# Wider weight casts and subtractions, and a shorter step of the S5 scan, in a two-layer hybrid diffusion step

## The chip, the core and the metric

The kernel runs on one core of one Trainium2 chip. The metric is device time in microseconds (us), the median of timed runs. TensorE (PE) multiplies matrices, VectorE (DVE) and ScalarE (ACT) do elementwise work, GpSimd (POOL) does small setups and issues DMAs, and SP issues the DMAs of the weights.

## The reference

The reference is one inference step of a small model with two layers, a width of 2048, and two streams of 128 tokens each (context and latent). All data are float32. Each layer does:

```python
h = rms_norm(x, norm_w) * (1 + scale) + shift          # adaLN: shift, scale, gate = c @ w_mod
hg..., at..., s5_u, s5_g, merge = split_columns(h @ w_in)   # 2048 x 15872
o_hg = hgrn2(...)          # gated linear recurrence, both directions
o_at = attention(...)      # 8 query heads, 2 key heads
o_s5 = s5(...)             # diagonal complex state space, both directions, 64 groups x 64 states
merged = g_hg * (o_hg @ w_br_hg) + g_at * (o_at @ w_br_at) + g_s5 * (o_s5 @ w_br_s5)
x = x + gate * (merged @ w_out)
```

The S5 branch runs, in each direction, `state[t+1] = a * state[t] + b[t]` with complex numbers; the new states of all branches are outputs too.

## The kernel before

**Weights.** Every large product goes through `gemm` (line 160). A weight matrix comes from HBM in pieces of 128 x 1024 float32 (512 KB), which hold two chunks of 128 rows by 512 columns. SP loads a piece into `raw` (three buffers, line 167). For each of the two halves, ScalarE casts it to the matmul's format, `wh`, and VectorE subtracts, `wl = raw - wh`, the remainder (`split_from`, lines 137 to 139). There are four buffers of 512 columns for each of `wh` and `wl` (the pool `weights`, line 68). PE then does six matmuls of 512 columns with a half: for each of the two streams lo x wh, hi x wh and hi x wl (lines 178 to 180), where hi and lo are the two parts of the activations, split in the same way. Sums stand in PSUM.

**The order.** Instructions carry priorities (the constants `P_...`, where a lower number goes first), and a planner of the framework lays down at build time the order of each engine, by its own estimate of when each instruction is ready. The order is then fixed. HGRN2 and attention come first (`P_MIX`), then the scan (`P_SCAN`), then the weights' loads, casts and subtractions (`P_TOP`), the layer's chain of small steps (`P_CHAIN`), the rest of S5 (`P_S5`), and last the weight matmuls (`P_PE`). The products of adaLN (`mod_part`, line 272) run as side work between weight matmuls: four column blocks of 256 side by side in the array, with weights of their own (`wm`), also loaded by SP.

**The S5 scan.** `s5_quarter` (line 782) does a quarter of the groups at a time. Two tokens are one step, so there are NP = 64 steps, over 8 quarters in the two layers: 512 steps. The states of both directions, real and imaginary parts, are 64 numbers a partition. A step (lines 822 to 831) has four VectorE operations, all 64 wide: the states times the real part of the coefficient (line 825), the swapped states times the signed imaginary part (line 827), the sum of both products (line 830), and the addition to the next input (line 831). The coefficients stand in a table `s5sc` of 384 numbers that `s5_params` writes once a layer (lines 693 to 703). `p` is a ring of four buffers for the products.

Ahead of a quarter's scan POOL sets up: it negates one half of C (line 791), copies four blocks into CC (line 762) and copies the initial state (line 804).

Of the kernel before, what the change touches and what calls it, by code (L numbers as in the profile page):

```python
# [11 lines left out]
F32R = mybir.dt.float32r  # L12
# [3 lines left out]
ALU = mybir.AluOpType  # L16
# [45 lines left out]
class Builder:  # L62
    def __init__(self, tc, ctx, io):
        self.tc, self.nc, self.io = tc, tc.nc, io
        self.seq = 0
        pool = lambda name, bufs, **kw: ctx.enter_context(tc.tile_pool(name=name, bufs=bufs, **kw))
        self.cp = pool("const", 1)
        self.wp = pool("weights", 4)
        self.sb = pool("sb", 1)
        self.bufs = dict(H8=4, Z8=2, Bl=1, CC=1, S16=1, uT=1, U2=1, ys=1, q4=2, kv=2,  # L70
                         mo=1, st=10, k2=6, k4=3, gt=4, sm=18, s5i=4, p=4, sb=1, sc=1, s5t=1)
        self.pg = pool("pg", 4, space=PSUM)
        self.pm = pool("pm", 2, space=PSUM)
        self.pb = pool("pb", 2, space=PSUM)
        self.dr = pool("scratch", 1, space=DRAM)
        self.uid = 0
# [51 lines left out]

# [1 line left out]
    def transpose4(self, src, n=4, ps=None):  # L130
# [29 lines left out]
    def gemm(self, pieces, hi, lo, nk):  # L160
        """hi(k), lo(k): [128, 256] stationary parts of both streams; pieces: DRAM APs [128, 1024]."""
        nc = self.nc
        ps = [self.pg.tile([128, 512], F32, tag="g", name=self.nm("g")) for _ in range(2)]
        for kk, src in enumerate(pieces):
            self.side_work()
            with self.prio(P_TOP):
                raw = self.wp.tile([128, 2, 512], F32, tag="raw", name=self.nm("raw"), bufs=RAW)
                nc.sync.dma_start(raw, src.rearrange("p (a b) -> p a b", a=2))
            for j in range(2):
                with self.prio(P_TOP):  # L170
                    wh = self.wp.tile([128, 512], F32R, tag="wh", name=self.nm("wh"))
                    wl = self.wp.tile([128, 512], F32R, tag="wl", name=self.nm("wl"))
                    self.split_from(raw[:, j], wh, wl)
                k = 2 * kk + j
                with self.prio(P_PE):
                    for s in range(2):
                        sl = slice(s * 128, s * 128 + 128)
                        nc.tensor.matmul(ps[s], lo(k)[:, sl], wh, start=(k == 0), stop=False)  # L178
                        nc.tensor.matmul(ps[s], hi(k)[:, sl], wh, start=False, stop=False)  # L179
                        nc.tensor.matmul(ps[s], hi(k)[:, sl], wl, start=False, stop=(k == nk - 1))  # L180
        return ps

    def rstd(self, ssq, n, width):
        """1/sqrt(ssq/width + eps), with one Newton step after the table's square root."""
        nc = self.nc
# [12 lines left out]

# [1 line left out]
    def condition(self):  # L200
# [41 lines left out]

# [1 line left out]
    def mod_part(self, l, part, prio, tags, plan):  # L244
        """A sixth of c @ w_mod for both streams, two k chunks at a time; four column blocks side by side.

        Parts 0 to 3 are shift and scale of a quarter of the channels, 4 and 5 the halves of the gate. plan: runs
        of chunk pairs that are summed in PSUM, (bank, pairs, pairs between two yields)."""
        nc, io = self.nc, self.io
# [46 lines left out]

# [1 line left out]
    def square(self, ssq, x, s, n):  # L298
# [9 lines left out]
    def normed(self, x, rs, q):  # L308
        """Channels 512 q .. 512 q + 511 of both streams."""
        nc = self.nc  # L310
# [20 lines left out]
    def in_group(self, l, name, idx, k0=0, k1=16):  # L331
        """Channel chunks k0 .. k1 - 1 of one group of columns."""
        pieces = [self.io["w_in"][l, GIDX[name, idx], kk] for kk in range(k0 // 2, k1 // 2)]
# [7 lines left out]
    def begin(self, l, name, idx, q):  # L341
        """A quarter of the channels' share of a group, put where the whole will stand."""
        ps = self.in_group(l, name, idx, 4 * q, 4 * q + 4)
# [40 lines left out]

# [1 line left out]
    def hgrn_unit(self, l, s, hf, q, f, v, og):  # L386
        """Four heads of one stream. q, f[2] (sigmoids), v: [128 tokens, 512]; og: output slice [128, 512].

        Pairs (s, t) are covered by a binary tree over time: at level m the queries of one half of every
        2m-block meet the keys of the other half; QF/KB carry the decay from the block's inner edge."""  # L390
        nc, io = self.nc, self.io
# [97 lines left out]

# [1 line left out]
    def head_norm(self, x, nh, w):  # L491
# [22 lines left out]
    def attention(self, l, s, q, kv, og):  # L514
        """q: [128, 8, 128], kv: [128, 512] (2 key heads, 2 value heads); og: [128, 1024]."""
        nc, io = self.nc, self.io
# [57 lines left out]

# [1 line left out]
    def vexp(self, x, n, wk):  # L576
        """exp on the vector engine to float32 accuracy."""
        nc = self.nc
# [60 lines left out]
    def s5_params(self, l):  # L639
        """Discretised per-state coefficients of both directions.  # L640

        The scan runs over pairs of tokens: state' = a^2 state + (a B u_first + B u_second)."""
        nc, io = self.nc, self.io
# [48 lines left out]
        cmul(acr, aci, abr, abi, cr, ci)  # L692
        sc = self.const(f"s5sc{l}", (128, 384))
        o = lambda off, ds: view(sc, off, ds)
        for qd in range(4):
            for d in range(2):
                i = qd * 2 + d
                pm = lambda c: view(c, d * 32 + qd * 8, [[1, 2], [2, 2], [4, 2]])
                for ri in range(2):
                    nc.vector.tensor_copy(o(i * 16 + ri * 8, [[4, 2], [2, 2], [1, 2]]), pm(a2r))  # L700
                    for st in range(2):
                        ts(o(128 + i * 32 + ri * 16 + st, [[8, 2], [4, 2], [2, 2]]), pm(a2i), 2.0 * ri - 1.0, None, ALU.mult)
        self.s5sc[l] = sc

    def s5_input(self, l, qd, Bl, C, Sb):
        """Input matrices of one quarter, block-diagonal over two groups, the odd token's part stacked on the
        even one's; built in the scan's buffer before the scan needs it."""
        nc, io = self.nc, self.io
# [34 lines left out]
    def s5_output(self, l, qd, C, CC, cb):  # L743
        """C a of both directions, and C B + diag(d), which joins a token to its own output."""
        nc = self.nc
# [18 lines left out]
    def s5_half(self, l, hh, us, ys):  # L764
        """Channels of chunks 4*hh .. 4*hh+3 of both streams; us[s]: [128 tokens, 512]."""
        nc = self.nc
# [15 lines left out]
    def s5_quarter(self, l, hh, qh, uT, U2, ys):  # L782
# [37 lines left out]
        with self.prio(P_SCAN):  # L820
            for i in range(NP):
                p0 = self.t("p", "p0", (128, 2, 32))
                p1 = self.t("p", "p1", (128, 2, 32))
                ds = DD + NP - 2 * i
                tt(p0.rearrange("p d (j s) -> p d j s", s=2), view(sc, qd * 32, [[16, 2], [1, 16], [0, 2]]),  # L825
                   view(Sb, i, [[ds, 2], [2 * W, 16], [W, 2]]), ALU.mult)
                tt(p1, view(sc, 128 + qd * 64, [[32, 2], [16, 2], [1, 16]]),  # L827
                   view(Sb, i + RI, [[ds, 2], [-RI, 2], [W, 16]]), ALU.mult)
                cur = view(Sb, i + 1, [[ds - 2, 2], [W, 32]])
                tt(p0, p0, p1, ALU.add)  # L830
                tt(cur, cur, p0, ALU.add)  # L831
        with self.prio(P_S5):
# [22 lines left out]

# [1 line left out]
    def layer(self, l, x, rs):  # L857
# [247 lines left out]
def _tiles(w, ncol):  # L1105
    """[K, N] -> [N/ncol, K/256, 128, 2*ncol]: 128-row chunks in pairs, side by side."""
    k, n = w.shape
# [4 lines left out]
def _mod_parts(w):  # L1112
    """Columns shift | scale | gate -> quarters of shift and scale together, halves of the gate."""
    h = D // 4
# [91 lines left out]
```

## Time and profile before

| | before |
|---|---|
| median of 3 timed runs | 2419.5 us (2418.51 to 2420.97) |
| span of the profiled execution | 2418.4 us (the page gives no time beside the span) |
| instructions | 38199 |
| PE busy | 2355.8 us, 97% |
| VectorE busy | 1812.5 us, 75% |
| ScalarE busy | 1185.1 us, 49% |
| POOL busy | 132.9 us, 5% |
| casts of weights (line 138) | 1344, 823.1 us |
| subtractions for weights (line 139) | 1344, 916.0 us |
| four operations of the scan (lines 825, 827, 830, 831) | 512 each; 140.1, 138.2, 112.8, 140.8 us |

All rows come from one profiled execution. Busy time is the time in which an engine has an instruction in work. Matmuls overlap: a 512-wide one shows about 0.40 us, and the next starts 0.23 us after it. A wait names the instruction that waited and what released it.

### The profile page before, as it was taken

Reading aid. Unit: us, or ns where it says so; the run is one execution under the profiler, and the core shown is the slowest. Engines: PE = TensorE matmul, PEld = TensorE weight load, DVE = VectorE, ACT = ScalarE, POOL = GpSimd, SP = SyncE. Lnnn points to the kernel's source line nnn. Section 1 sums busy time; section 2 is a strip of 40 time slices with the busy share of each in tenths; the row PEclk is TensorE's granted clock in tenths of the full one; section 3 lists DMA queues with packets and bytes.
Section 4 is the critical chain, followed back from the end, with each engine's and each line's share of the span. In section 5 each row is a group of like instructions: output and inputs, shape, how many; then the busy total and the mean of one; then the engine's idle time right before and its main releaser. Section 6 shows DMA issues by size and latency. Waiting matters only on the chain.

```text
span 2418.4 us, 38199 instructions
## 1 busy us (share of the span) xinstructions
PE 2355.8 (97%) x13192; PEld 1817.0 (75%) x13192; DVE 1812.5 (75%) x4835; ACT 1185.1 (49%) x2061; POOL 132.9 (5%) x244
## 2 busy tenths in 40 slices
PE   5999999999999999999998999999999999999997
PEld 2667878888786676677776888888888776687776
DVE  5855998799878768665565798899869868856555
ACT  3436645555553433444446555555564453354444
POOL 2000001000100100000010001000010010000000
PEclk9999999999999999999999999999999999999999
DMA  8994553345557767777864554354546656656665
GB/s 311 344 326 133 161 181 115 124 155 192 170 164 261 238 212 252 243 270 252 298 214 143 158 175 153 126 166 149 184 157 191 198 166 211 219 174 219 224 199 177
DMA packets 131490, 483.85 MB, mean 200 GB/s; under 512 B 17200, under 2 KB 17808, under 8 KB 126944
## 3 DMA queue, kind: packets, MB, share of 16 engines
q1 hardware_dynamic: 120528, 454.09, 57.0%
q0 software_dynamic: 9472, 23.97, 3.4%
q10 hardware_dynamic: 1296, 3.36, 0.4%
q8 instruction: 103, 1.69, 0.3%
q14 instruction: 91, 0.75, 0.1%
HBM read 474.36 MB, written 6.98 MB: 199 GB/s over the span
## 4 chain that ended last, share of the span: by engine, by line
PE 92%; DMA 3%; DVE 3%; issue 1%; ACT 1%; SPq 0%; DVEq 0%; ACTq 0%
PE g L178 26%; PE g L180 25%; PE g L179 25%; PE mod L272 5%; PE bu L813 2%; PE lv L429 2%; DMA raw<-w_in 2%; PE tr L134 2%; PE yp L844 1%; DVE wl L139 1%; DMA wm<-w_mod 1%; PE yp L837 1%; PE bt L731 1%; PE ao L569 0%; PE sc L553 0%
## 5 line engine op out<-in xcount | busy, mean ns | idle before, releaser
L138 ACT CAST wh<-raw 128x512 fp32r<-128x512 f32 x1344 | 823.1, 621 | 1005.9 <-PE g L179 759.5
L139 DVE TENSOR_TENSOR wl<-raw,wh 128x512 fp32r<-128x512 f32 x1344 | 916.0, 688 | 418.2 <-ACT wh L138 365.6
L178 PE MATMUL g<-wh,hl 128*128 128x512 f32 x1984 | 798.2, 402 | 4.9 <-ACT wh L138 2.4
L179 PE MATMUL g<-wh,hh 128*128 128x512 f32 x1984 | 787.4, 397 | 0.0
L180 PE MATMUL g<-wl,hh 128*128 128x512 f32 x1984 | 716.6, 404 | 0.0
L178 PEld LDWEIGHTS g<-wh,hl 128*128 128x128 f32 x1984 | 375.1, 189 | 117.7 <-ACT wh L138 17.8
L180 PEld LDWEIGHTS g<-wl,hh 128*128 128x128 f32 x1984 | 366.0, 189 | 97.4 <-DVE Sb L831 6.6
L179 PEld LDWEIGHTS g<-wh,hh 128*128 128x128 f32 x1984 | 375.3, 189 | 81.8 <-issue 0.4
L272 PE MATMUL mod<-wm,cs 128*32 128x256 f32 x1536 | 155.6, 406 | 22.8 <-DMA wm<-w_mod 16.2
L178 PE MATMUL g<-wh,ol 128*128 128x512 f32 x384 | 154.5, 402 | 0.0
L825 DVE TENSOR_TENSOR p<-s5sc,Sb 128x64 f32<-128x64 f32 x512 | 140.1, 274 | 16.1 <-ACT Sb L817 7.1
L179 PE MATMUL g<-wh,oh 128*128 128x512 f32 x384 | 150.1, 391 | 0.0
L831 DVE TENSOR_TENSOR Sb<-Sb,p 128x64 f32<-128x64 f32 x512 | 140.8, 275 | 8.7
L827 DVE TENSOR_TENSOR p<-s5sc,Sb 128x64 f32<-128x64 f32 x512 | 138.2, 270 | 0.0
L180 PE MATMUL g<-wl,oh 128*128 128x512 f32 x384 | 133.9, 394 | 0.0
L272 PEld LDWEIGHTS mod<-wm,cs 128*32 128x32 f32 x1536 | 50.0, 113 | 106.8 <-issue 54.9
L830 DVE TENSOR_TENSOR p<-p,p 128x64 f32<-128x64 f32 x512 | 112.8, 220 | 6.4
L178 PE MATMUL g<-wh,mt 128*128 128x512 f32 x256 | 101.6, 397 | 0.0
L179 PE MATMUL g<-wh,mt 128*128 128x512 f32 x256 | 101.1, 395 | 0.0
L178 PEld LDWEIGHTS g<-wh,ol 128*128 128x128 f32 x384 | 72.0, 188 | 26.1 <-ACT wh L138 7.7
L180 PE MATMUL g<-wl,mt 128*128 128x512 f32 x256 | 85.4, 400 | 1.2 <-DVE wl L139 1.2
L180 PEld LDWEIGHTS g<-wl,oh 128*128 128x128 f32 x384 | 71.2, 188 | 18.7 <-DVE Sb L831 1.6
(315 smaller groups left out, 2112.6 us busy)
## 6 DMA issues: line engine op xcount, KB each, us to landing
raw<-w_in SPq DMA_DIRECT2D x496, 512.0 KB, 3.8
wm<-w_mod SPq DMA_DIRECT2D x130, 512.0 KB, 5.1
raw<-w_br SPq DMA_DIRECT2D x96, 512.0 KB, 4.2
raw<-w_out SPq DMA_DIRECT2D x64, 512.0 KB, 4.4
wm<-w_mod SPq DMA_DIRECT2D x31, 1024.0 KB, 7.4
raw<-w_glu SPq DMA_DIRECT2D x16, 512.0 KB, 4.3
gb<-gate_d POOLq DMA_DIRECT2D x16, 256.0 KB, 6.4
x<-x ACTq DMA_DIRECT2D x2, 1024.0 KB, 14.4
```

What stands on the lines that cost most here:

```text
L134: nc.tensor.transpose(ps[:, k], src[:, k * 128:(k + 1) * 128], self.ident)
L138: self.nc.scalar.copy(hi, src)
L139: self.nc.vector.tensor_sub(lo, src, hi.bitcast(F32))
L178: nc.tensor.matmul(ps[s], lo(k)[:, sl], wh, start=(k == 0), stop=False)
L179: nc.tensor.matmul(ps[s], hi(k)[:, sl], wh, start=False, stop=False)
L180: nc.tensor.matmul(ps[s], hi(k)[:, sl], wl, start=False, stop=(k == nk - 1))
L272: nc.tensor.matmul(ps[32 * i:32 * i + 32, 0:256], self.cT[:, 2 * k:2 * k + 32], ws[k - 2 * k0][:, i * 256:i * 256 + 256], start=(k == 2 * kb),
L429: nc.tensor.matmul(ps[:, h], mix[:, h], view(Z, HT + h * 128, [[2 * m, nb], [2 * HT + m, 2], [1, m]]), start=True, stop=True)
L825: tt(p0.rearrange("p d (j s) -> p d j s", s=2), view(sc, qd * 32, [[16, 2], [1, 16], [0, 2]]), view(Sb, i, [[ds, 2], [2 * W, 16], [W, 2]]) ...
L827: tt(p1, view(sc, 128 + qd * 64, [[32, 2], [16, 2], [1, 16]]), view(Sb, i + RI, [[ds, 2], [-RI, 2], [W, 16]]), ALU.mult)
L830: tt(p0, p0, p1, ALU.add)
L831: tt(cur, cur, p0, ALU.add)
```

## The change

The weights are cast and subtracted a whole piece at a time, 1024 wide, with three buffers for each of `wh` and `wl`; the matmuls read the halves of these. In the scan both products are one operation of 128 elements, whose inputs are read twice; the coefficient table is laid out for it (512 numbers), and its sum reads the second product with its halves swapped. The ring `p` has three larger buffers. The build call sets `dynamic_dma_scratch_size`. Comments are taken out. The core of the diff:

```diff
-        self.wp = pool("weights", 4)
+        self.wp = pool("weights", 3)
...
-                         mo=1, st=10, k2=6, k4=3, gt=4, sm=18, s5i=4, p=4, sb=1, sc=1, s5t=1)
+                         mo=1, st=10, k2=6, k4=3, gt=4, sm=18, s5i=4, p=3, sb=1, sc=1, s5t=1)
...
+            with self.prio(P_TOP):
+                wh = self.wp.tile([128, 2, 512], F32R, tag="wh", name=self.nm("wh"))
+                wl = self.wp.tile([128, 2, 512], F32R, tag="wl", name=self.nm("wl"))
+                self.split_from(raw, wh, wl)
             for j in range(2):
-                with self.prio(P_TOP):
-                    wh = self.wp.tile([128, 512], F32R, tag="wh", name=self.nm("wh"))
-                    wl = self.wp.tile([128, 512], F32R, tag="wl", name=self.nm("wl"))
-                    self.split_from(raw[:, j], wh, wl)
...
-                        nc.tensor.matmul(ps[s], lo(k)[:, sl], wh, start=(k == 0), stop=False)
+                        nc.tensor.matmul(ps[s], lo(k)[:, sl], wh[:, j], start=(k == 0), stop=False)
...
-        sc = self.const(f"s5sc{l}", (128, 384))
+        sc = self.const(f"s5sc{l}", (128, 512))
...
-                    nc.vector.tensor_copy(o(i * 16 + ri * 8, [[4, 2], [2, 2], [1, 2]]), pm(a2r))
                     for st in range(2):
-                        ts(o(128 + i * 32 + ri * 16 + st, [[8, 2], [4, 2], [2, 2]]), pm(a2i), 2.0 * ri - 1.0, None, ALU.mult)
+                        at = qd * 128 + d * 32 + ri * 16 + st
+                        nc.vector.tensor_copy(o(at, [[8, 2], [4, 2], [2, 2]]), pm(a2r))
+                        ts(o(at + 64, [[8, 2], [4, 2], [2, 2]]), pm(a2i), 1.0 - 2.0 * ri, None, ALU.mult)
...
-                p0 = self.t("p", "p0", (128, 2, 32))
-                p1 = self.t("p", "p1", (128, 2, 32))
+                p = self.t("p", "p", (128, 2, 2, 32))
                 ds = DD + NP - 2 * i
-                tt(p0.rearrange("p d (j s) -> p d j s", s=2), view(sc, qd * 32, [[16, 2], [1, 16], [0, 2]]),
-                   view(Sb, i, [[ds, 2], [2 * W, 16], [W, 2]]), ALU.mult)
-                tt(p1, view(sc, 128 + qd * 64, [[32, 2], [16, 2], [1, 16]]),
-                   view(Sb, i + RI, [[ds, 2], [-RI, 2], [W, 16]]), ALU.mult)
+                tt(p, view(sc, qd * 128, [[64, 2], [32, 2], [1, 32]]), view(Sb, i, [[0, 2], [ds, 2], [W, 32]]), ALU.mult)
                 cur = view(Sb, i + 1, [[ds - 2, 2], [W, 32]])
-                tt(p0, p0, p1, ALU.add)
-                tt(cur, cur, p0, ALU.add)
+                own = p[:, 0]
+                tt(own, own, view(p, 80, [[32, 2], [-16, 2], [1, 16]]), ALU.add)
+                tt(cur, cur, own, ALU.add)
...
-    nc = bacc.Bacc("TRN2", target_bir_lowering=False, num_devices=1)
+    nc = bacc.Bacc("TRN2", target_bir_lowering=False, num_devices=1, dynamic_dma_scratch_size=4096)
```

## Rows read from the trace of the kernel before

**Rows 1.** The page: span, then busy time, share and count of PE.

```profile
span 2418.4 us, 38199 instructions
...
PE 2355.8 (97%) x13192; PEld 1817.0 (75%) x13192; DVE 1812.5 (75%) x4835; ACT 1185.1 (49%) x2061; POOL 132.9 (5%) x244
```

**Rows 2.** Waits of PE, whole run: us in total, times, longest.

```profile
PE tr L134 <- DVE xn L319: 10.3, 3, 6.4
...
PE g L178 <- ACT wh L138: 2.4, 5, 1.2
...
PE g L180 <- DVE wl L139: 1.2, 2, 0.9
...
PE bu L813 <- ACT Bl L732: 0.4, 1, 0.4
```

**Rows 3.** Busy time of each engine in two windows, clock, DMA share.

```profile
700.00:750.00 50.00, 50.00 (x243) 38.55 (x241) 46.56 (x141) 23.87 (x41) 0.00 (x0) 1.00 0.70 228
...
1100.00:1150.00 50.00, 50.00 (x263) 37.45 (x260) 25.64 (x41) 20.28 (x35) 0.00 (x0) 1.00 0.77 253
```

**Rows 4.** Waits of ScalarE's casts, whole run.

```profile
ACT wh L138 <- PE g L179: 759.5, 834, 3.7
...
ACT wh L138 <- DMA raw<-w_in: 83.9, 35, 11.8
```

**Rows 5.** Groups by form: busy us, mean ns of one, then idle before.

```profile
L139 DVE TENSOR_TENSOR wl<-raw,wh 128x512 fp32r<-128x512 f32 x1344 | 916.0, 688 | 418.2 <-ACT wh L138 365.6 <-PE g L180 34.2 <-ACT Sb L817 2.8
L138 ACT CAST wh<-raw 128x512 fp32r<-128x512 f32 x1344 | 823.1, 621 | 1005.9 <-PE g L179 759.5 <-DMA raw<-w_in 83.9 <-DVE wl L139 58.2
...
L830 DVE TENSOR_TENSOR p<-p,p 128x64 f32<-128x64 f32 x512 | 112.8, 220 | 6.4
...
L501 DVE TENSOR_TENSOR q<-q,qnorm 128x1024 f32<-128x1024 f32 x4 | 4.9, 1220 | 0.0
```

**Rows 6.** Timeline of VectorE: one step of the scan (start, us, operation).

```profile
390.62 0.28 DVE L825 TENSOR_TENSOR p<-s5sc,Sb 128x64 f32<-128x64 f32 x1
390.81 0.27 DVE L827 TENSOR_TENSOR p<-s5sc,Sb 128x64 f32<-128x64 f32 x1
...
391.69 0.27 DVE L825 TENSOR_TENSOR p<-s5sc,Sb 128x64 f32<-128x64 f32 x1
```

**Rows 7.** Timeline: two subtractions and two casts of weights back to back.

```profile
304.19 1.27 DVE L139 TENSOR_TENSOR wl<-raw,wh 128x512 fp32r<-128x512 f32 x2
...
1256.71 1.14 ACT L138 CAST wh<-raw 128x512 fp32r<-128x512 f32 x2 [3.43 <-DMA raw<-w_out]
```

**Rows 8.** Timeline of PE: a short visit of adaLN between weight matmuls.

```profile
749.21 0.39 PE L178 MATMUL g<-wh,ol 128*128 128x512 f32 x1
749.44 0.39 PE L179 MATMUL g<-wh,oh 128*128 128x512 f32 x1
749.76 0.62 PE L272 MATMUL mod<-wm,cs 128*32 128x256 f32 x2
750.31 0.73 PE L180 MATMUL g<-wl,oh 128*128 128x512 f32 x2
```

**Rows 9.** Windows, line 272 alone: busy time of PE and PEld.

```profile
50.00:200.00 150.00, 25.70 (x384) 10.02 (x384) 0.98 0.82 294
...
700.00:1000.00 300.00, 48.46 (x416) 14.81 (x416) 1.00 0.72 237
...
1050.00:1250.00 200.00, 23.95 (x288) 9.05 (x288) 1.00 0.78 266
...
1900.00:2110.00 210.00, 26.45 (x160) 6.32 (x160) 1.00 0.61 199
```

**Rows 10.** Waits of the weight loader, first in 700:1000, then in 1900:2110.

```profile
PEld mod L272 <- issue: 16.6, 46, 0.4
...
PEld mod L272 <- issue: 14.5, 40, 0.4
```

**Rows 11.** Groups: the POOL operation on C, all eight.

```profile
L791 POOL TENSOR_SCALAR C<-C 128x256 f32<-128x256 f32 x8 | 10.9, 1364 | 6.7 <-DMA C<-s_c 6.6
```

**Rows 12.** Timeline of POOL: the first of these.

```profile
24.45 0.88 POOL L791 TENSOR_SCALAR C<-C 128x256 f32<-128x256 f32 x1
```

More of the change, by code (lines that the diff above doesn't have):

```diff
@@ L177, in gemm @@
                         sl = slice(s * 128, s * 128 + 128)
-                        nc.tensor.matmul(ps[s], lo(k)[:, sl], wh, start=(k == 0), stop=False)
-                        nc.tensor.matmul(ps[s], hi(k)[:, sl], wh, start=False, stop=False)
-                        nc.tensor.matmul(ps[s], hi(k)[:, sl], wl, start=False, stop=(k == nk - 1))
+                        nc.tensor.matmul(ps[s], lo(k)[:, sl], wh[:, j], start=(k == 0), stop=False)
+                        nc.tensor.matmul(ps[s], hi(k)[:, sl], wh[:, j], start=False, stop=False)
+                        nc.tensor.matmul(ps[s], hi(k)[:, sl], wl[:, j], start=False, stop=(k == nk - 1))
         return ps
@@ L696, in s5_params @@
             for d in range(2):
-                i = qd * 2 + d
                 pm = lambda c: view(c, d * 32 + qd * 8, [[1, 2], [2, 2], [4, 2]])
                 for ri in range(2):
-                    nc.vector.tensor_copy(o(i * 16 + ri * 8, [[4, 2], [2, 2], [1, 2]]), pm(a2r))
                     for st in range(2):
-                        ts(o(128 + i * 32 + ri * 16 + st, [[8, 2], [4, 2], [2, 2]]), pm(a2i), 2.0 * ri - 1.0, None, ALU.mult)
+                        at = qd * 128 + d * 32 + ri * 16 + st
+                        nc.vector.tensor_copy(o(at, [[8, 2], [4, 2], [2, 2]]), pm(a2r))
+                        ts(o(at + 64, [[8, 2], [4, 2], [2, 2]]), pm(a2i), 1.0 - 2.0 * ri, None, ALU.mult)
         self.s5sc[l] = sc
```

## The prediction

> **What bounds the kernel now.** I read the engines' busy times first, to see which engine has no slack: PE is busy 2355.8 of 2418.4 us [rows 1], so 62.6 us of the span are its idle time. The waits of PE say what for [rows 2]: 2.4 us for a cast weight (wh), 1.2 us for a weight remainder (wl), 10.3 us for the normalised input (xn) at the layers' starts; most of the rest is the first weights' arrival and what follows the last matmul. Waits for the two things that this change makes cheaper are therefore 3.6 us in 2418. Then the windows, for the share of VectorE by stage [rows 3]: 46.56 us of 50 where the S5 scan runs, 25.64 where it doesn't, and PE is at 50.00 in both. Last the waits of ScalarE [rows 4]: before 834 casts it stood 759.5 us until PE gave a weight buffer back, and only 83.9 us for a weight's DMA. Casts run ahead of PE and are held by PE, not PE by casts. PE's queue is the bound, and its length is the number of matmuls, the stalls, and what it costs to change from one kind of matmul to another.
>
> **The change part by part.**
>
> *Casts and subtractions 1024 wide.* 1344 casts and 1344 subtractions become 672 and 672. A subtraction of 512 takes 0.688 us alone [rows 5], two back to back 1.27 [rows 7]; a VectorE operation of 1024 on two float32 inputs took 1.22 [rows 5]. That saves 0.05 to 0.16 us a pair, 672 times: 34 to 104 us of VectorE. A cast of 1024 has no row. Below it lies 0.62 us (one of 512), above 1.24 (two of 512 apart); two back to back take 1.14 [rows 7], so the second adds 0.52, and I take 1.06, near that row. ScalarE is relieved by 672 x 0.08 = 54 us, by the bounds -67 to 417. All of this lies beside PE's matmuls, whose number and shape don't change: it is worth 0 on the path, except through the stalls and the order below.
>
> *The scan.* Four operations become three: two multiplications of 64 become one of 128, the two additions stay. A step now takes 1.07 us, from one first operation to the next (390.62 to 391.69 [rows 6]); the second multiplication starts 0.19 after the first. A 64-wide operation takes 0.220 and a 1024-wide one 1.220 [rows 5], 1.04 ns an element, so the wide multiplication adds 0.07 to the 0.28 of the first one. Bounds: 0 (one price for both) to 0.28 (twice the price). I take 0.07: 1.07 - 0.19 + 0.07 = 0.95, 0.12 us saved a step, 512 steps, 61 us of VectorE; by the bounds +0.19 to -0.09 a step, 97 us gained to 46 lost. The scan is not on PE's path: PE fills its time with weight matmuls meanwhile, so 0 again. If that cover were gone, the whole 61 us would count.
>
> *Three buffer pairs.* Four halves become three whole pieces, six halves. PE consumes a half in 6 matmuls, about 1.39 us (0.23 us from start to start [rows 8]); PE can go on for 8.3 instead of 5.6 us on what is cast when a weight comes late. The stalls for wh and wl (3.6 us) should nearly all go: -3, bounds -3.6 and 0.
> Against it stands the coarser grain: where the buffers ran empty, the first half waits for a cast of 1.06 instead of 0.62 and for a subtraction of 1.22 instead of 0.69, +0.44 to +0.97 an event. The seven waits in rows 2 would give +3 to +7 if the deeper buffers saved none; I take +1 for two that remain. Behind a wide subtraction on VectorE stand the operations that the layer's start needs (the longest wait for xn is 6.4 us [rows 2]); one that comes just behind it is 0.5 us later, and two layer starts have it: within the same +1. The raw buffers stay at three, so the first three DMAs of the run are the same. The smaller area named in the build call touches POOL's DMAs alone; they wait for engines, not for each other, and I cost it at 0 (one late gate load in the last column block would cost its whole delay).
>
> *The order on PE.* The planner lays PE's order down at build time, and it sees the new times. Here lies the largest term. The adaLN matmuls (line 272) are put between weight matmuls. In a run of 16 they cost 0.067 us each: 25.70 us for 384 in 50:200. In 700:1000 it is 48.46 for 416, in 1050:1250 23.95 for 288, in 1900:2110 26.45 for 160 [rows 9]. At 0.067 those 864 would take 57.9 us instead of 98.9: 41 us of PE go on short visits. In 1900:2110 the weight loader stood before such a visit 40 times, four matmuls a visit; in 700:1000 46 times [rows 10]. One visit shows where they come from [rows 8]: after the last matmul on wh (749.44) PE turns to two adaLN matmuls for 0.55 us, and only then to the two on wl. In the plan wl was late, and the gap was filled. Visits are short where VectorE is full by rows 3, longer in 1050:1250 where it is not. With one wl for 12 matmuls instead of one for 6, and a shorter scan step, there are fewer such gaps. Bounds: -41 us (all visits whole) and +44 (all 864 at the 0.165 of 1900:2110). I take -8, a fifth of the excess: only visits that stand between wh and wl can go, their matmuls must still run, and the planner may put other gaps in their place.
>
> **The sum.** -3 + 1 - 8 = -10 us on the profiled execution: 2408.4 us of span. The page gives that execution no time beside its span; the median of the timed runs (2419.5) is 1.1 us more. So 2409.5, rounded to 2410 us, 0.4% faster.
>
> **A rule of the skill that speaks against it.** A POOL operation that reads SBUF (line 791) took 0.88 us at 24.45 us, before VectorE had its first weight to subtract [rows 12], and 1.364 on average [rows 11]. The Trainium skill, "SBUF — State Buffer", section "Who interferes with whom", says that a VectorE instruction with two SBUF inputs blocks a GpSimd instruction that reads SBUF until it has finished. The trace agrees so far as the two figures differ by 0.48 us, less than one subtraction of 0.688; what this would give is the second rival below.
>
> **The rivals.**
> *PE-bound, order unchanged.* The relief of VectorE and ScalarE is hidden, the adaLN visits stay as they are, and 3.6 us of waits is all there was to win. For it: PE at 50.00 of 50, with VectorE full and with VectorE half idle. Against it: a planner that sees other times seldom gives the same order. -3 + 1 = -2: 2417.5 us. The same time comes out where the wide operations cost twice the narrow ones, so that the change doesn't do what it says.
> *A longer hold on VectorE that blocks POOL.* A wide subtraction lasts 0.53 us more than a narrow one. In each of the 8 S5 quarters seven POOL reads stand ahead of the scan or its output (the negation of C, four copies into CC, two of the initial state): 7 x 0.53 = 3.7 us later, 30 us in all if PE had run out of weight matmuls each time. It hasn't: of these I'd expect a third, +10, less 2 for the stalls and with no gain of order: 2427.5 us. It decides only from the point where PE waits for bu or yp; such a wait is 0.4 us in all today.
> *A worse order (slower).* The two casts' work comes in one lump of 12 matmuls, and the planner fills in adaLN, S5 and HGRN2 matmuls in more and shorter visits. Place: 700:1250 and 1900:2110. Price: the 2-matmul visit of rows 8 puts 0.87 us between two weight matmuls that otherwise start 0.23 apart, and two matmuls in a run of 16 take 0.13: 0.51 us for the visit itself. With 20 more such visits +10, less 2 for the stalls: 2427.5 us. It decides from 4 more visits on, where they cost the 2 us of the stalls. For it: each earlier gap was filled because a matmul was ready, and adaLN weights come in two halves. Against it: two wh come together now, so PE has eight matmuls to do before wl is missed, not four.
>
> **How the numbers follow.** Forecast 0.54; no change of order 0.24 (0.05 of it that wide operations save nothing); worse order 0.17; POOL blocked 0.05. About 0.2% (4.8 us) is what can be told from no change. The forecast's own range is 2397 to 2414: order terms of -20 to -4. The time falls below 2395 where more than half of the excess of 41 us goes, 0.08, and above 2427 in about half of the worse cases, 0.11; so 2395 to 2427. Faster: 0.54 less the part of the forecast that ends within 4.8 us, plus a little of the unchanged order that also gains: 0.54. Same 0.25, slower 0.21.
>
> **What would show it.** Line 139 at 1.22 us x672 and line 138 near 1.06 x672; a scan step of 0.95 us from start to start. PE's waits for wh and wl under 1.5 us together. PE's sum of waits otherwise as before, at the start, between the layers (6.4 us for xn) and behind the last matmul. Line 272 in the scan stages of both layers cheaper than 0.1165 and 0.165 us a matmul, and fewer than 46 and 40 waits of the weight loader before it. The order step is wrong if these counts stay or rise; then the gain is 2 us at most. The whole is wrong if VectorE's relief shows up as idle time of VectorE and PE's busy time grows.

## The result, and the profile after

| | before | after |
|---|---|---|
| median | 2419.0 us (4 runs beside these) | 2388.2 us (2385.4 to 2389.9, 4 runs) |
| ratio | | 0.9871, interval 0.9857 to 0.9885 |
| span of the profiled execution | 2418.4 us | 2388.1 us |
| span less PE's busy time | 62.6 us | 68.0 us |

The kernel became 1.3% faster. The direction was forecast, the size was not: 2410 was said, and 2388.2 lies below the range of 2395 to 2427.

The page of after, for [rows 1]:

```profile
span 2388.1 us, 35164 instructions
...
PE 2320.1 (97%) x13192; PEld 1820.5 (76%) x13192; DVE 1743.4 (73%) x3683; ACT 1077.4 (45%) x1392; POOL 137.7 (6%) x244
```

PE shows the same 13192 records of matmuls in 35.7 us less of busy time, while its idle time grew by 5.4 us. So nothing was won from waits. Its waits in after, for [rows 2] (in total, times, longest):

```profile
PE mod L272 <- DMA wm<-w_mod: 21.0, 11, 5.0
PE tr L134 <- DVE xn L319: 17.6, 4, 7.7
...
PE st L484 <- ACT kts L481: 3.1, 2, 1.6
...
PE g L178 <- ACT wh L138: 1.1, 2, 0.5
PE g L180 <- DVE wl L139: 0.8, 1, 0.8
```

The weights' casts and remainders now cost 1.9 us for 3.6 before. Against that the adaLN weights (`wm`) cost more than in the kernel before, whose row is

```profile
PE mod L272 <- DMA wm<-w_mod: 16.2, 8, 4.9
```

The busy time went down at line 272. Windows of after with line 272 alone (PE busy, then PEld), for [rows 9]:

```profile
50.00:200.00 150.00, 26.56 (x384) 10.19 (x384) 0.95 0.80 292
700.00:1000.00 300.00, 34.34 (x418) 14.04 (x418) 1.00 0.72 247
1050.00:1250.00 200.00, 17.11 (x256) 7.51 (x256) 0.99 0.80 274
1900.00:2110.00 210.00, 17.14 (x128) 4.69 (x128) 1.00 0.61 203
```

At the start little changed. In 700:1000 a record costs 0.082 us for 0.1165, in 1050:1250 0.067 for 0.083, in 1900:2110 0.134 for 0.165. The weight loader's waits before such a visit, first in 700:1000, then in 1900:2110, for [rows 10]:

```profile
PEld mod L272 <- issue: 9.3, 26, 0.4
...
PEld mod L272 <- issue: 8.7, 24, 0.4
```

26 and 24 for 46 and 40. The groups of after, for [rows 5, 11]:

```profile
L139 DVE TENSOR_TENSOR wl<-raw,wh 128x1024 fp32r<-128x1024 f32 x672 | 821.5, 1223 | 435.3 <-ACT wh L138 413.2 <-PE g L180 13.2 <-PE bt L731 3.1
...
L138 ACT CAST wh<-raw 128x1024 fp32r<-128x1024 f32 x672 | 705.1, 1050 | 972.0 <-PE g L179 727.7 <-DMA raw<-w_in 93.5 <-DMA raw<-w_out 33.5
...
L824 DVE TENSOR_TENSOR p<-s5sc,Sb 128x128 f32<-128x128 f32 x512 | 202.6, 396 | 16.6 <-ACT Sb L817 5.0
...
L272 PE MATMUL mod<-wm,cs 128*32 128x256 f32 x1536 | 128.4, 404 | 27.6 <-DMA wm<-w_mod 21.0 <-DVE cs L207 6.6
...
L791 POOL TENSOR_SCALAR C<-C 128x256 f32<-128x256 f32 x8 | 11.0, 1370 | 6.5 <-DMA C<-s_c 6.4
```

Line 272 takes 27.2 us less over the whole run. In the kernel before its row is

```profile
L272 PE MATMUL mod<-wm,cs 128*32 128x256 f32 x1536 | 155.6, 406 | 22.8 <-DMA wm<-w_mod 16.2 <-DVE cs L207 6.5
```

The unbroken step of the scan, for [rows 6] (start, us, operation):

```profile
346.49 0.39 DVE L824 TENSOR_TENSOR p<-s5sc,Sb 128x128 f32<-128x128 f32 x1
346.91 0.23 DVE L827 TENSOR_TENSOR p<-p 128x64 f32<-128x64 f32 x1
347.17 0.28 DVE L828 TENSOR_TENSOR Sb<-Sb,p 128x64 f32<-128x64 f32 x1
347.49 0.39 DVE L824 TENSOR_TENSOR p<-s5sc,Sb 128x128 f32<-128x128 f32 x1
```

1.00 us for 1.07. And ScalarE's casts still stand until PE gives a buffer back, 727.7 us of their idle time where it was 759.5 [rows 4]: PE is as much the bound as it was.

**What a visit costs.** A visit is an unbroken run of line 272 between other matmuls. The code holds 768 adaLN matmuls (2 layers x 6 parts x 16 chunks x 4 column blocks), the trace 1536 records: one column block is two records, the four blocks side by side are eight. The rest can be read from timelines of PE. In after, one block alone:

```profile
751.20 0.39 PE L179 MATMUL g<-wh,oh 128*128 128x512 f32 x1
751.52 0.62 PE L272 MATMUL mod<-wm,cs 128*32 128x256 f32 x2
752.07 0.73 PE L180 MATMUL g<-wl,oh 128*128 128x512 f32 x2
```

All four blocks, in the run with two wide pairs (experiment e3):

```profile
908.20 0.64 PE L272 MATMUL mod<-wm,cs 128*32 128x256 f32 x8
```

Four blocks twice, in the kernel before:

```profile
1096.24 0.40 PE L179 MATMUL g<-wh,hh 128*128 128x512 f32 x1
1096.56 1.07 PE L272 MATMUL mod<-wm,cs 128*32 128x256 f32 x16
1097.57 0.73 PE L180 MATMUL g<-wl,hh 128*128 128x512 f32 x2
```

Four blocks four times, in the run with six narrow halves (e6):

```profile
755.39 0.39 PE L180 MATMUL g<-wl,oh 128*128 128x512 f32 x1
755.71 1.93 PE L272 MATMUL mod<-wm,cs 128*32 128x256 f32 x32
757.57 0.50 PE L178 MATMUL g<-wh,ol 128*128 128x512 f32 x1
757.91 0.40 PE L179 MATMUL g<-wh,oh 128*128 128x512 f32 x1
```

One block costs 0.62 us and four cost 0.64: a round of blocks has one price, however many of the four are in it. From the weight matmul ahead to the one behind it is 0.87, 1.33 and 2.18 us for one, two and four rounds, where 0.23 would pass without a visit, and the first matmul behind lasts 0.11 longer (757.57 to 757.91 is 0.34; a pair shows 0.73 where two in sequence show 0.62). So a visit costs 0.75, 1.21 and 2.06 us: **0.31 a visit and 0.44 a round**, an estimate from these rows. Counted over the whole timeline of PE, with a round for each eight records or part of them (the ratio is to the kernel before, timed beside each run at 2418.8 to 2420.8 us):

| kernel | median us, ratio (interval) | PE busy | span less PE busy | visits (of at most 4 records) | rounds | 0.31 x visits + 0.44 x rounds |
|---|---|---|---|---|---|---|
| before | 2419 | 2355.8 | 62.6 | 169 (94) | 266 | 169.4 |
| after | 2388.2, 0.9871 (0.9857 to 0.9885) | 2320.1 | 68.0 | 102 (40) | 230 | 132.8 |
| e1 before + scan | 2422.5, 1.001 (1.000 to 1.002) | 2357.2 | 63.8 | 169 (92) | 267 | 169.9 |
| e2 after, old scan | 2401.8, 0.9921 (0.9906 to 0.9936) | 2327.9 | 72.1 | 108 (43) | 233 | 136.0 |
| e3 after, two pairs | 2406.9, 0.9945 (0.993 to 0.9959) | 2331.2 | 75.0 | 130 (29) | 227 | 140.2 |
| e4 before, adaLN first | 2363.4, 0.9766 (0.9751 to 0.978) | 2294.8 | 65.6 | 88 (3) | 195 | 113.1 |
| e5 after, adaLN last | 2492.6, 1.0303 (1.0287 to 1.0318) | 2385.1 | 106.1 | 185 (116) | 286 | 183.2 |
| e6 before, six halves | 2357.3, 0.9743 (0.9729 to 0.9758) | 2289.4 | 66.2 | 62 (1) | 194 | 104.6 |
| e7 e6 + scan | 2359.6, 0.9754 (0.9739 to 0.9768) | 2290.9 | 67.4 | 60 (0) | 193 | 103.5 |
| e8 after, adaLN first | 2368.4, 0.9787 (0.9771 to 0.9804) | 2297.5 | 68.7 | 93 (9) | 201 | 117.3 |
| e9 before, five halves | 2374.1, 0.9819 (0.9805 to 0.9834) | 2306.5 | 65.5 | 81 (18) | 212 | 118.4 |
| e10 before, seven halves | 2367.8, 0.979 (0.9776 to 0.9805) | 2296.4 | 68.4 | 59 (1) | 193 | 103.2 |
| e11 before, half of adaLN | 2373.6, 0.9811 (0.9794 to 0.9827) | 2280.3 | 91.7 | 90 (46) | 129 | 84.7 |
| e12 after, half of adaLN | 2359.4, 0.9757 (0.9742 to 0.9771) | 2281.3 | 75.3 | 91 (47) | 131 | 85.8 |

From before to after the last column falls by 36.6 us and PE's busy time by 35.7. Between before and the other runs that keep all of adaLN the two changes agree within 7 us, but for e5.

### The profile page after: what moved, and what is told of

The parts are those of the page before. It is cut to its first block, busy times and chain, and to the rows that moved or that the text cites. A ratio compares the mean times of both kernels' runs of the same rounds, so it can differ in the third digit from the quotient of the medians.

```text
span 2388.1 us, 35164 instructions
## 1 busy us (share of the span) xinstructions
PE 2320.1 (97%) x13192; PEld 1820.5 (76%) x13192; DVE 1743.4 (73%) x3683; ACT 1077.4 (45%) x1392; POOL 137.7 (6%) x244
## 4 chain that ended last, share of the span: by engine, by line
PE 94%; DMA 3%; DVE 2%; ACT 1%; issue 1%; SPq 0%; DVEq 0%; ACTq 0%
PE g L180 26%; PE g L178 26%; PE g L179 26%; PE mod L272 4%; PE bu L813 2%; PE lv L429 2%; PE tr L134 2%; DMA wm<-w_mod 1%; PE yp L841 1%; DMA raw<-w_in 1%; PE bt L731 1%; PE yp L834 1%; DMA raw<-w_br 1%; PE ao L569 0%; PE sc L553 0%
## 5 line engine op out<-in xcount | busy, mean ns | idle before, releaser
L138 ACT CAST wh<-raw 128x1024 fp32r<-128x1024 f32 x672 | 705.1, 1050 | 972.0 <-PE g L179 727.7
L139 DVE TENSOR_TENSOR wl<-raw,wh 128x1024 fp32r<-128x1024 f32 x672 | 821.5, 1223 | 435.3 <-ACT wh L138 413.2
L180 PE MATMUL g<-wl,hh 128*128 128x512 f32 x1984 | 767.9, 402 | 0.8 <-DVE wl L139 0.8
L824 DVE TENSOR_TENSOR p<-s5sc,Sb 128x128 f32<-128x128 f32 x512 | 202.6, 396 | 16.6 <-ACT Sb L817 5.0
L272 PE MATMUL mod<-wm,cs 128*32 128x256 f32 x1536 | 128.4, 404 | 27.6 <-DMA wm<-w_mod 21.0
L180 PE MATMUL g<-wl,oh 128*128 128x512 f32 x384 | 142.9, 394 | 0.0
L827 DVE TENSOR_TENSOR p<-p 128x64 f32<-128x64 f32 x512 | 114.3, 223 | 11.2
L180 PE MATMUL g<-wl,mt 128*128 128x512 f32 x256 | 94.0, 396 | 0.0
L178 PEld LDWEIGHTS g<-wh,ol 128*128 128x128 f32 x384 | 72.1, 188 | 19.4 <-issue 2.7
L180 PEld LDWEIGHTS g<-wl,oh 128*128 128x128 f32 x384 | 71.3, 188 | 18.4 <-issue 2.9
L179 PEld LDWEIGHTS g<-wh,oh 128*128 128x128 f32 x384 | 72.1, 188 | 15.0 <-issue 0.4
```

The lines of the kernel that those rows point to most:

```text
L138: self.nc.scalar.copy(hi, src)
L139: self.nc.vector.tensor_sub(lo, src, hi.bitcast(F32))
L178: nc.tensor.matmul(ps[s], lo(k)[:, sl], wh[:, j], start=(k == 0), stop=False)
L179: nc.tensor.matmul(ps[s], hi(k)[:, sl], wh[:, j], start=False, stop=False)
L180: nc.tensor.matmul(ps[s], hi(k)[:, sl], wl[:, j], start=False, stop=(k == nk - 1))
L272: nc.tensor.matmul(ps[32 * i:32 * i + 32, 0:256], self.cT[:, 2 * k:2 * k + 32], ws[k - 2 * k0][:, i * 256:i * 256 + 256], start=(k == 2 * kb),
```

## The experiments

In the expectations a departure is a change on PE from a weight matmul to another kind; theory O says that the planned order of PE carries the gain.

**e1_scan_only.** The kernel before with the new scan alone (and the build call of after).

```diff
-                tt(p0..., view(sc, qd * 32, ...), view(Sb, i, ...), ALU.mult)
-                tt(p1, view(sc, 128 + qd * 64, ...), view(Sb, i + RI, ...), ALU.mult)
+                tt(p, view(sc, qd * 128, [[64, 2], [32, 2], [1, 32]]), view(Sb, i, [[0, 2], [ds, 2], [W, 32]]), ALU.mult)
```

> The scan with three operations alone; weights cast and subtracted 512 wide with four buffers each, as before. PE's planned order leaves the weight matmuls 389 times (before 385, after 308), 161 times for adaLN (160, 98). Theory O (the gain of 31 us is shorter PE order: 35.7 us of PE busy time for 77 fewer exits, 0.46 us each): 2419 + 2 = 2421 us, no gain. Rival R (the gain is the relief of VectorE, to which the scan gives a part as large as the subtractions): about 2404 us.

2422.5 us: no gain. The step fell from 1.064 to 1.000 us (medians of the unbroken steps), and the visits stayed as they were, 169 with 267 rounds. The shorter scan by itself neither reaches the path nor moves the order.

**e2_wide_only.** The other part alone: wide operations and three pairs, old scan.

```diff
-        self.wp = pool("weights", 4)
+        self.wp = pool("weights", 3)
...
+                self.split_from(raw, wh, wl)
```

> Wide casts and subtractions with three buffer pairs alone; the scan keeps its four operations. Planned exits 308, for adaLN 101. O: the whole gain, 2388 us. R: the part of the scan is missing, about 2403 us.

2401.8 us, the rival's figure. The visits fall to 108, nearly to those of after, and PE's busy time by 27.9. On top of this the scan is worth 12 us to after by the ratios (13.6 by the medians): 7.8 of busy time, 4.1 of idle time. One edit alone gives nothing, and beside the other about two fifths of the whole; the parts don't add up.

**e3_wide_two_pairs.** After with two pairs, that is four halves, as before.

```diff
-        self.wp = pool("weights", 3)
+        self.wp = pool("weights", 2)
```

> All of the change, but two buffer pairs in place of three: as many halves as before. Planned exits 342, for adaLN 122. O: 2388 + 34 x 0.46 = 2404 us, half of the gain gone though every operation is as wide as in the changed kernel. R (the wide operations carry it, the number of buffers does little): 2388 to 2391 us.

2406.9 us: some 13 of the 31 us are left without the third pair. Short visits are even fewer than in after (29), but visits are more (130), and PE waits for the coarse pieces:

```profile
PE g L178 <- ACT wh L138: 9.6, 8, 1.6
...
PE g L180 <- DVE wl L139: 8.8, 11, 2.1
```

18.4 us for 1.9 in after. This is the grain's cost that the prediction put at +1; three pairs do away with it.

**e4_before_adaln_first.** The kernel before, buffers, casts and scan untouched; the adaLN matmuls get a priority ahead of the weight matmuls.

```diff
-                        yield from self.mod_part(*p, P_PE, tags, [("m", MB, MB)] * (8 // MB))
+                        yield from self.mod_part(*p, P_CHAIN, tags, [("m", MB, MB)] * (8 // MB))
```

(and the same for `L - 1, p`)

> The kernel before with one edit: the side matmuls of adaLN get the priority of the layer's chain instead of that of the weight matmuls, so that the planner runs all that are ready at once. Casts, buffers and scan as before. Planned exits 291, for adaLN 69. O: 2419 - 94 x 0.46 = 2376 us if each exit counts alike, 2380 to 2390 if adaLN's are cheaper than the rest. R (VectorE's load decides, and it is unchanged): 2419 us.

2363.4 us, 25 us ahead of after and 13 under the lowest figure of theory O. Once an adaLN piece may start, it goes through: 3 short visits for 94, 195 rounds, where 192 is the least. The page of e4:

```profile
PE 2294.8 (97%) x13192; PEld 1816.2 (77%) x13192; DVE 1806.9 (77%) x4835; ACT 1182.3 (50%) x2060; POOL 130.5 (6%) x244
```

With VectorE's and ScalarE's work as before, PE's busy time falls by 61.0 us; the visits' price falls by 56.3. So the order suffices, and no relief of VectorE is needed for it.

**e5_after_adaln_late.** After, with adaLN behind the weight matmuls: the gain should go if it is the order.

```diff
-                        yield from self.mod_part(*p, P_PE, tags, [("m", MB, MB)] * (8 // MB))
+                        yield from self.mod_part(*p, P_PE + 1000, tags, [("m", MB, MB)] * (8 // MB))
```

> The changed kernel with one edit: the side matmuls of adaLN get a priority 1000 behind the weight matmuls', so that the planner uses them as fillers. Casts, three buffer pairs and scan as changed. Planned exits from the weight matmuls 380 (changed kernel 308, before 385), for adaLN 178 (98, 160), 107 of them of one matmul. O (PE's order carries the gain): the gain is gone, 2388 + 13 for the exits + about 30 for adaLN's own matmuls = 2431 us, though every operation is wide. R (the relief by wide operations and the deeper buffers act on the chip itself): 2388 to 2395 us.

2492.6 us. The whole gain is gone: 185 visits, 116 of them short, 286 rounds, 50 us more than in after by their price. Another 54 us came on top that nothing had foreseen, 38 of them as idle time of PE. PE's waits in e5:

```profile
PE mod L272 <- DMA wm<-w_mod: 42.0, 26, 5.0
```

21 us more: the adaLN weights hold their buffers longer (SP stands 167.5 us before it may load such a piece, 94.1 in after) and come late. A further 14 us lie behind PE's last matmul. That is one of adaLN in e5 and one of the weights in after (timelines of PE):

```profile
2462.44 1.05 PE L272 MATMUL mod<-wm,cs 128*32 128x256 f32 x10
...
2374.34 0.40 PE L180 MATMUL g<-wl,mt 128*128 128x512 f32 x1
```

From its end to the end of the span 27.7 us pass in e5, since the last gate has yet to be written and loaded, and 13.4 in after. The other 15 us are busy time beyond the visits' price. One window of e5 (PE, PEld, DVE, ACT, POOL busy, then the granted clock):

```profile
1000.00:1500.00 500.00, 466.93 (x2449) 340.62 (x2448) 279.04 (x480) 199.23 (x268) 26.16 (x47) 0.95 0.68 225
```

PE stands 33 us in it and the granted clock is 0.95, so part of it ran at the lower of the two levels (1.2 for 2.4 GHz) after PE had stood; after shows 0.99 there. How much of the 15 us that makes isn't shown. The run shows the order's direction, not its price.

**e6_narrow_six.** The kernel before with six half buffers instead of four: the room of three pairs, narrow operations, old scan (build call as in after).

```diff
-        self.wp = pool("weights", 4)
+        self.wp = pool("weights", 6)
```

> The kernel before with six 512-wide buffers each for wh and wl in place of four; casts, subtractions and scan as before, the smaller scratch area as in the change. Planned exits 277, for adaLN 55. O with depth as the cause of the order: a larger gain than the change's, 2419 - 18 (exits) - 42 (adaLN in whole runs) = 2359 us. R (wide operations are what helps): 2415 to 2419 us.

2357.3 us, the best of all, 31 us ahead of after. The page of e6:

```profile
PE 2289.4 (97%) x13192; PEld 1820.7 (77%) x13192; DVE 1805.3 (77%) x4835; ACT 1177.0 (50%) x2059; POOL 133.1 (6%) x244
...
L272 PE MATMUL mod<-wm,cs 128*32 128x256 f32 x1536 | 104.4, 401 | 25.1 <-DMA wm<-w_mod 18.6
```

VectorE and ScalarE work as long as before, and PE is busy 66.4 us less. One short visit is left of 94. At equal room and with the same old scan the wide operations of e2 cost 44 us against these narrow ones.

**e7_narrow_six_scan.** e6 with the new scan, as in e1.

> As the run with six narrow buffers, with the scan of three operations too. Planned exits 265, for adaLN 56. O: 2356 us, 2 below the run without the scan for 12 exits fewer. R: it is slower than the changed kernel (2388 us) by what narrow operations cost, 2395 to 2419 us.

2359.6 us: the intervals of e6 and e7 overlap. Where the order is good already, the scan has nothing to give. Against after, which differs from e7 by the wide grain alone, it is 29 us ahead.

**e8_after_adaln_first.** After, with the edit of e4.

> The changed kernel with adaLN's side matmuls at the priority of the layer's chain (as in e4). Planned exits 276, for adaLN 67; 291 and 69 in e4. O: what the change gained is nearly all contained in e4, so 2388 - 20 - 5 = 2363 us, the same as e4 within 5. R (wide operations, deeper buffers and adaLN's order add up): 2363 - 31 = 2332 us.

2368.4 us. Wide grain and scan bring nothing beyond e4 (2363.4); both ways of mending the order mend the same thing.

**e9_narrow_five** and **e10_narrow_seven.** As e6, with 5 and 7.

> The kernel before with five instead of four half buffers of each kind, narrow casts and the old scan. Theory O (the halves cast ahead shape the planned order, and the adaLN visits and the departures from weight matmuls set the time): the plan holds 298 departures, 72 of them for adaLN (385 and 160 before; 277 and 55 with six halves, which took 2357). At 0.196 us a departure (15.1 us of weight-matmul time for the 77 that the changed kernel lost) that is -17 us; adaLN time as in the runs with 67 and 69 departures for it, 87 to 88 us for 128, is -40; stalls +3: 2365 us, 2360 to 2371. Rival D (the time falls with each half buffer, whatever the order): half of the 62 us that six halves gave: 2388 us, 2383 to 2393.

> The kernel before with seven half buffers of each kind, narrow casts and the old scan. Theory O: the plan holds 266 departures, 52 for adaLN, hardly fewer than with six halves (277 and 55): adaLN time has nothing more to give (85 us), 11 departures give -2: 2355 us, 2351 to 2359. Rival D (each half buffer gives 31 us): 2326 us.

2374.1 and 2367.8 us. Up to six halves the time falls with the visits: the first buffer gives 45 us, the next 17. The seventh takes 10 back, with no more visits and rounds than six, so neither theory covers it. Both times lie above theory O's own ranges, by 3 and by 9 us. For e9 the adaLN part was taken from runs with fewer rounds (212 here, 195 and 201 there). In e10 PE is idle 2 us longer than in e6 and busy 7 us longer, and of these 6.7 stand at two lines of S5 (lines 813 and 844, 112.3 us for 105.6). PE waits 3.1 us for the end of a scan there (0.6 in e6), and around that wait, from 991 to 998, the granted clock is 0.52. Why seven halves lead to this order stays open.

**e11_before_little_adaln** and **e12_after_little_adaln.** These two leave out 384 of the 768 adaLN matmuls, a half and not most, as the expectation has it. PE's busy time falls by 75.5 us from before to e11, where 114 were expected, and its idle time grows by 29; so both times are above 2305.

```diff
                     for k in range(2 * k0, 2 * (k0 + burst)):
                         for i in range(4):
+                            if prio == P_PE and k != 2 * kb:
+                                continue
```

> The kernel before without most of the adaLN sums that are spread through the layers: of each run of chunk pairs only the first chunk's four matmuls are left, all weights are still loaded. Taken with the next kernel, which leaves out the same of the changed kernel. Its plan holds 313 departures from weight matmuls, 86 for adaLN; the next one's 294 and 86. Theory O (the gain lies in the adaLN visits and the departures): about 75 fewer adaLN visits of a plan and fewer columns give some 2419 - 14 (72 departures at 0.196) - 100 (most of the 128 us of adaLN time) = 2305 us, 2290 to 2320; the next kernel then differs by 19 departures, -4, and 5 us more stalls: within -6 to +4 us of this one. Rival W (the wide casts and the shorter scan serve the weight matmuls themselves, adaLN or not): the next kernel keeps at least 13 us of the 31 us of gain.

> The changed kernel without the same adaLN sums as the run before: 294 departures from weight matmuls, 86 for adaLN. Theory O: -6 to +4 us beside that run, some 2305 us. Rival W: at least 13 us less than that run.

2373.6 and 2359.4: 14.2 us apart, outside theory O's -6 to +4 and on the rival's side of its line. The table says which way. Visits, rounds and PE's busy time are alike (2280.3 and 2281.3), as theory O has it: where the visits are equal, PE's work is. The difference is idle time, 91.7 and 75.3 us. PE's waits in e11:

```profile
PE g L178 <- ACT wh L138: 12.3, 15, 2.4
PE yp L846 <- DVE Sb L833: 10.9, 1, 10.9
PE tr L134 <- DVE xn L321: 10.4, 3, 6.5
PE bt L733 <- ACT Bl L734: 6.5, 1, 6.5
```

and in e12:

```profile
PE tr L134 <- DVE xn L321: 17.7, 4, 8.0
PE g L178 <- ACT wh L138: 7.9, 13, 1.0
```

With less adaLN to fill PE, S5 shows at last in e11: 10.9 us for the end of a scan and 6.5 for S5's set-up. In e12 neither wait is left. So the change is worth something off the order as soon as the cover is thin; whether the shorter scan or the wide operations do it these two runs don't separate. In the full kernel the cover is there (0.4 us is the longest wait for S5 [rows 2]), and neither e1 nor e7 gained.

## Why the prediction was wrong

**Right.** PE is the bound, and its waits are no prize. Subtraction 1.223 us (1.22 said), cast 1.050 (1.06 said), and both hidden. The direction, and the place: line 272 cheaper in each window of the scan stages, fewer waits of the weight loader. The changed order as the largest term. The rival of the unchanged order falls with 102 visits for 169, that of the worse order too. The rival of POOL falls on its condition: PE never waits for bu or yp in after. The block itself is there. In after the operation on C takes 0.85 us while VectorE stands, and 1.33 where a wide subtraction had begun 0.60 us before it (POOL and VectorE, timelines of after):

```profile
1718.85 0.85 POOL L791 TENSOR_SCALAR C<-C 128x256 f32<-128x256 f32 x1 [0.50 <-DMA C<-s_c]
...
965.02 1.23 DVE L139 TENSOR_TENSOR wl<-raw,wh 128x1024 fp32r<-128x1024 f32 x1 [0.66 <-ACT wh L138]
...
965.62 1.33 POOL L791 TENSOR_SCALAR C<-C 128x256 f32<-128x256 f32 x1 [3.06 <-DMA C<-s_c]
```

It ends 0.70 us after the subtraction does, so most of its own work had to wait. This bears out the sentence of the Trainium skill, "SBUF — State Buffer", section "Who interferes with whom", that went with the rival. The mean of the eight hardly moves (1370 ns for 1364): in either kernel three take under 0.9 us and five, which meet such operations of VectorE, 1.20 to 2.53.

**The step that failed: "I take -8, a fifth of the excess: only visits that stand between wh and wl can go".** The order was worth about -36: PE's busy time fell by 35.7. Two things were wrong in the step.

The first is which visits go. I had one row of a visit between `wh` and `wl` [rows 8] and took it for the kind. The kernel before has 63 visits between wh and wl, 36 of them of at most 4 records, and 89 between a half's last `wl` and the next half's `wh`, 54 of them short. In after the short ones are 39 of 56 and 0 of 33. The short ones that I said could go stayed, and those that I had not counted went. In e6 both kinds are gone (0 of 9 and 0 of 33); in e1 both are there (24 of 51 and 65 of 104). The bound of -41 for all of them stood in the prediction; a count by neighbours would have replaced the fifth.

The second is the price. I took a matmul's mean in long runs (0.067 us a record) and so reckoned with line 272's busy time alone. A round of four blocks costs 0.44 whether it is full or not, and each visit 0.31 beside that, in part in the weight matmuls' times: line 272's own busy time fell by 27.2 of the 35.7 us. 67 visits at 0.31 and 36 rounds at 0.44 are 36.6 us. What the prediction counts as matmuls of line 272 are records, two for each matmul, so its four a visit are two.

**Cause and credit.** I put the better order down to one wl for 12 matmuls and to a shorter step of the scan. Shown is: halves cast ahead decide most (e6: two more halves give 62 us, and the build call that goes with them gained nothing in e1; e3: without the third pair only some 13 are left), the scan alone nothing (e1), beside wide casts some 12 us (e2), and the wide grain costs 29 us at equal room (e7 against after; 44 with the old scan, e6 against e2). How the planner's estimates lead to these orders a trace doesn't show. That wide pieces leave the visits before `wl`, because a whole remainder of 1.22 us must end before the first half's third kind of matmul may start, fits the counts and is argued only.

**Smaller terms.** Stalls -3 + 1: the waits for wh and wl fell from 3.6 to 1.9 us, not under 1.5, and other waits ate it up, `wm` +4.8, `st` +3.1 and xn +7.3, the longest 7.7 us and not 6.4; one of 5.7 us before a transpose (line 134) is gone. PE's idle time in all +5.4. The scan's step 1.00 for 0.95 said: the wide multiplication took 396 ns where the first one had 274. The prediction added 0.07 for 64 more elements; it is 0.12. The casts cost ScalarE 118 us less, not 54: the sum sets the wide cast against two back to back (1.14), while two cost 1.24 on the average, and its bounds mix the two bases. It is off the path.

## What to carry to other kernels

When PE is the bound at 97% and its waits are small, look at the order on it: list the visits of each kind of matmul by length and by what stands before and behind, and price a whole visit from the weight matmul ahead to the one behind. How many pieces are ready ahead changed here how many gaps the planner filled; buffers in small pieces gave more than the same room in large ones, up to six. Try the priority or the buffer count alone before a change that mixes it with something else: e4 and e6, edits of one priority and of one buffer count, gave about twice what the whole change gave.

## What the runs showed of the hardware

Column blocks of 32 side by side are paid by the round: x2, x4, x6 and x8 records at 0.62 to 0.64 us, x16 at 1.07, x32 at 1.93. A split round is paid twice. The Trainium skill, "TensorEngine Tiling (Array Packing)", section "Key Properties", says that tiles work independently and that changing the tiling mode drains TensorE. The rows agree with both. The 0.31 us of a visit, the rounds aside, is what the way there and back costs here, and the prediction did not weigh it. Visits by matmuls over the whole array, which change no mode, have no such price in the kernel before:

```profile
422.15 0.39 PE L179 MATMUL g<-wh,hh 128*128 128x512 f32 x1
422.38 1.03 PE L731 MATMUL bt<-ident,Sb 128*128 128x128 f32 x8
423.18 0.71 PE L180 MATMUL g<-wl,hh 128*128 128x512 f32 x2
...
214.24 0.39 PE L179 MATMUL g<-wh,hh 128*128 128x512 f32 x1
214.47 0.60 PE L731 MATMUL bt<-ident,Sb 128*128 128x128 f32 x4
214.82 0.71 PE L180 MATMUL g<-wl,hh 128*128 128x512 f32 x2
```

Reckoned as above they cost 0.89 us for eight records and 0.44 for four: 0.11 a record and nothing beside. That the 0.31 is the drain itself fits this, and no run here isolates it.

The multiplication of 128 elements in the new scan, whose states are read twice and with large strides, took 396 ns, and the first one of 64 in the old scan 274: 1.9 ns for each element more, while a subtraction of float32 costs 1.05 ((1223 - 688) / 512). Which feature of the reads makes it dear isn't shown.
